# Differential attention as sixteen steps with the projections in between, and own PSUM banks for scores and transposes

## The chip, the cores and the metric

The kernel runs on one core of one Trainium2 chip. The metric is the device time of the whole program in microseconds (us), as the median of several executions. One core has five engines that work side by side, each through its own queue in order: TensorE (PE, matrix products and transposes), VectorE (DVE), ScalarE (ACT), GpSimd (POOL) and SyncE (SP, which issues the DMAs).

## The reference, cut to what matters

A transformer block with differential attention, latent attention, memory cross-attention and a mixture of experts is followed by a second block (gated delta rule, sliding-window attention, two feed-forward layers). There are 512 tokens of width 1024. The change lies in the first stage, the mixer of the first block:

```
h = rms_norm(x, norm_mix_g); proj = h @ w_in
q_d, k_d, v_d, c_q, c_kv, k_pe = split(proj)
lam = exp(sum(lq1 * lk1)) - exp(sum(lq2 * lk2)) + lambda_init
# differential attention: 8 heads, two score maps of width 32 per head
p = softmax(s1 + bias) - lam * softmax(s2 + bias)      # causal; bias is linear in the distance of the positions
diff_out = rms_norm(p @ v_d) * gain
# latent attention follows, from c_q, c_kv and k_pe
x = x + concat([diff_out, mla_out]) @ w_out
```

The keys and values of the memory attention (`w_mem_kv` on a normed memory of 256 rows) are projected in this stage too, and are read in the next one.

## The kernel before

Activations are held with features on the 128 partitions and 512 tokens along the free axis, in 8 chunks. A projection is a product in three parts (`mm3`, L399 to L401): activations and weights are each split into a high and a low part in a reduced 32-bit format (`hi`, `lo`, `xh`, `xl`; ACT makes the high part at L406, DVE the low part at L407), and three products are accumulated for each of 8 chunks, 24 matmuls for one block. A block of 128 output columns streams 512 columns in each matmul; a block of `w_v` or of the memory streams 256. The weights come in tiles of 512 KB, issued by SP as buffers come free. The accumulators of the projections (`mmp`) turn over in two banks of PSUM.

`mix()` runs first: `start` makes the split of the normed activations and the sums of squares (`sqt`, then `stp` on PE, `rt` on POOL, `stb` on PE, `rbc` on DVE). Then `MSEQ` lists the parts in program order: `p` projects a pair of query and key blocks (4 pairs), `v` half of the values, `c` and `k` the latent blocks, `r` the rope table, `n` the latent norms, `m` the memory's load, keys and values, and `h` (`attend(c)`) the differential attention of a pair of heads. One `attend` has four parts, i = 0 to 3, of 128 queries against (i+1)*128 keys. A part makes four score maps (`sc`, L1857, each on 32 rows of PE's array), takes their minimum against the distance on DVE (`s`, L1861), scales the minimum (`mnd`, L1866), takes the exponentials on ACT (L1870), joins two maps per head (L1874 to L1876), transposes the result on PE (`pt`, L2014), copies it on ACT (`pT`, L2016) and multiplies it with the values (`po`, L2006). After four parts the output is normed and transposed (`on`, L1888; `pt`, L1892).

What stands on each engine in which order is settled by a scheduler that places all instructions by its own estimate of their times, with program order as the priority. So parts that are listed one after the other can be mixed with each other. PSUM has 8 banks. In this part of the program two go to the projections, one to `po`, and five (`ps_d`) are shared by the score maps, by the transposes and by the first pair's two projections (`PQ`). The first of those five is the bank in which `start` has its sums.

Of the kernel before, what the change touches and what calls it, by code (L numbers as in the profile page):

```python
# [13 lines left out]
P = 128  # L14
# [13 lines left out]
MSEQ="v0 p1 v1 h0 r0 p2 c0 h1 c1 p3 h2 k1 k0 n0 m0 h3 m1 m2"  # L28
# [249 lines left out]
class K:  # L278
# [1440 lines left out]
    def mix(self):  # L1719
# [5 lines left out]
        with ExitStack() as st:  # L1725
# [20 lines left out]
            def qk(j):  # L1746

                ps = self.proj(d["w_qk"], j, hs, bank=ps_d.tile([P, T], F32, name="po", tag="s") if j in PQ else None)
# [5 lines left out]
                return t  # L1754
# [3 lines left out]
            def pair(c):  # L1758
                return qk(c), qk(c + 4)

            self.cst_load(mp, "mix")
            nxt = pair(0)
# [41 lines left out]
            pairs, cq, kms, cqs, mem = {0: nxt}, [], [], [], []  # L1804

            def latent_q(j):
                ps = self.proj(d["w_qk"], 8 + j, hs)
                t = F(f"cq{j}")
                V.tensor_tensor(t, ps, rbc, OP.mult)
                cq.append(t)  # L1810

            def latent_kv():
                ps = self.proj(d["w_qk"], 10, hs)
                t = F("ckv")
                V.tensor_tensor(t, ps, rbc, OP.mult)
                return t

            def rope_keys():
                ps = self.proj(d["w_qk"], 11, hs)
                kp = F("kp")  # L1820
                V.tensor_tensor(kp, ps, rbc, OP.mult)
                V.tensor_tensor(kp, kp, cs, OP.mult)
# [6 lines left out]

            def latent_norms():  # L1830
# [3 lines left out]
                V.scalar_tensor_tensor(mq, bq, -(96.0 ** -0.5), cs, op0=OP.mult, op1=OP.mult)  # L1834
                rkv, bkv = self.stats([ckv], 128, B)
# [5 lines left out]
                self.split(t[:, 0], t[:, 1], ckv, self.sm("mla_kv_norm_g"))  # L1841
                return mq, rkv, bkv, (t[:, 0], t[:, 1])

            def attend(c):

                q, k = pairs[c]
                slopes = [2.0 ** -(2 * c + a + 1) for a in range(2)]
                po = ps_o.tile([P, 4, 2, 64], F32, name="po", tag="po")
                mn, sm = Y("mnd", 16), Y("smd", 16)

                sm = sm.rearrange("p (m i a) -> p m i a", m=2, a=2)
                for i in range(4):
                    n = (i + 1) * P
                    sc = [ps_d.tile([P, T], F32, name="sc", tag="s")[:, :n] for m in range(4)]
                    for m in range(4):
                        r = slice(32 * m, 32 * m + 32)
                        nc.tensor.matmul(sc[m], q[r, i * P:n], k[r, :n], start=True, stop=True)  # L1857
                    es = []
                    for m in range(4):
                        s = w3.tile([P, T], F32, name="s", tag="s")[:, :n]  # L1860
                        V.tensor_tensor_reduce(s, sc[m], dist[i], 1.0, 3e38, OP.add, OP.min,  # L1861
                                               mn[:, 4 * i + m:4 * i + m + 1])
                        es.append(s)
                        if m % 2:
                            mi = mn[:, 4 * i + m - 1:4 * i + m + 1]
                            V.tensor_scalar(mi, mi, slopes[m // 2], None, op0=OP.mult)  # L1866
# [181 lines left out]
```

## Time and profile before

| what | us |
|---|---|
| median of three timed executions (2113.8 to 2115.72) | 2114.2 |
| the profiled execution, its own time | 2121.12 |
| its span, first to last instruction | 2118.9 |
| PE busy in the span | 2008.4 |
| the stretch of the differential attention, first projection to last product with the values (24.9 to 265.3) | 240.4 |
| PE busy in that stretch | 208.72 |

All times of rows are us from the span's start. In the profile, a PE row's length includes the time until its result is out, so the cost of one matmul in a sequence is read from start to start. The granted clock of PE is given as a share of full speed: 1.00 is the 2.4 GHz level, 0.50 the 1.2 GHz level.

### The profile page before, as it was taken

To read this page: it belongs to the slowest core of one execution; us is meant where nothing else is said; L and a number is where in the kernel's file an instruction comes from. 1 tells how busy PE (TensorE), PEld (TensorE's weight loads), DVE (VectorE), ACT (ScalarE), POOL (GpSimd) and SP (SyncE) were. 2 spreads that over 40 slices of the span, in tenths; PEclk is the share of its full clock that TensorE was granted. 3 is DMA by queue.
4 is the path that set the end of the run, shared out by engine and by line. 5 is a ranking of instruction groups with operands and counts; after the bars stand their busy time and mean duration, and the time that the engine had idled before them with its cause. 6 is when DMAs were issued, how large, how long until landed. Compare 5 with 4: busy or idle time off the path is not lost.

```text
span 2118.9 us, 26396 instructions
## 1 busy us (share of the span) xinstructions
PE 2008.4 (95%) x10094; PEld 1539.6 (73%) x10094; DVE 1036.4 (49%) x2115; ACT 739.9 (35%) x1453; POOL 343.6 (16%) x320
## 2 busy tenths in 40 slices
PE   5988799989999999999999899999999999999997
PEld 5767567877555556787887788888877678888887
DVE  6455474663222325778875643344345654334334
ACT  4335464452111113344553422222324543222221
POOL 2001124120000000244440211011111011101111
PEclk9877799999999998999999999999999999999999
DMA  4212211426988874211112232332231023233322
GB/s 155 80 40 60 75 41 51 154 68 223 383 287 331 331 279 159 71 60 41 53 38 80 89 98 77 114 93 88 88 100 50 21 89 91 87 92 110 100 76 74
DMA packets 75457, 243.44 MB, mean 115 GB/s; under 512 B 8824, under 2 KB 11968, under 8 KB 75328
## 3 DMA queue, kind: packets, MB, share of 16 engines
q1 hardware_dynamic: 73520, 240.34, 33.8%
q8 instruction: 81, 1.33, 0.3%
q10 hardware_dynamic: 1664, 1.34, 0.2%
q14 instruction: 48, 0.39, 0.1%
q0 software_dynamic: 144, 0.04, 0.0%
HBM read 235.36 MB, written 6.29 MB: 114 GB/s over the span
## 4 chain that ended last, share of the span: by engine, by line
PE 70%; DVE 3%; ACT 1%; POOL 1%; DMA 1%; issue 0%; DVEq 0%; ACTq 0%
PE mmp L399 16%; PE mmp L400 16%; PE mmp L401 15%; PE pgu L1548 6%; PE psx L1614 3%; PE py L1548 3%; PE pgt L1564 3%; PE sc L1327 1%; PE po L748 1%; PE tp L961 1%; PE po L1353 1%; PE sc L728 1%; PE pt L1339 0%; DVE cv L949 0%; POOL sqt L433 0%; PE pg L968 0%
## 5 line engine op out<-in xcount | busy, mean ns | idle before, releaser
L399 PE MATMUL mmp<-xh,hi 128*128 128x512 f32 (+1 forms) x1328 | 523.5, 394 | 1.9 <-DVE g L805 1.1
L400 PE MATMUL mmp<-xl,hi 128*128 128x512 f32 (+1 forms) x1328 | 517.3, 390 | 0.9 <-DVE xl L410 0.9
L401 PE MATMUL mmp<-xh,lo 128*128 128x512 f32 (+1 forms) x1328 | 517.2, 389 | 0.0
L406 ACT ACTIVATE hi<-raw 128x1024 fp32r<-128x1024 f32 (+2 forms) x256 | 252.6, 988 | 663.5 <-PE mmp L400 587.7
L407 DVE TENSOR_TENSOR lo<-raw,hi 128x1024 fp32r<-128x1024 f32 (+1 forms) x242 | 279.7, 1157 | 149.3 <-ACT hi L406 145.1
L399 PEld LDWEIGHTS mmp<-xh,hi 128*128 128x128 f32 x1328 | 253.4, 191 | 57.5 <-issue 4.5
L400 PEld LDWEIGHTS mmp<-xl,hi 128*128 128x128 f32 x1328 | 253.2, 191 | 51.9 <-issue 2.5
L401 PEld LDWEIGHTS mmp<-xh,lo 128*128 128x128 f32 x1328 | 252.7, 190 | 50.5 <-issue 1.0
L807 POOL TENSOR_TENSOR g<-g,rbc 128x512 f32<-128x512 f32 x44 | 75.2, 1708 | 508.8 <-ACT g L806 508.8
L399 PE MATMUL mmp<-ahi,hi 128*128 128x512 f32 (+1 forms) x374 | 141.9, 380 | 0.0
L400 PE MATMUL mmp<-alo,hi 128*128 128x512 f32 (+1 forms) x374 | 141.9, 380 | 0.0
L401 PE MATMUL mmp<-ahi,lo 128*128 128x512 f32 (+1 forms) x374 | 141.9, 379 | 0.0
L433 POOL TENSOR_TENSOR sqt<-sqt 128x512 f32<-128x512 f32 (+1 forms) x50 | 68.6, 1373 | 245.0 <-ACT sqt L429 228.2
L809 DVE TENSOR_TENSOR a<-mmp,g 128x512 f32<-128x512 f32 x44 | 30.4, 691 | 144.6 <-PE mmp L401 144.6
L805 DVE TENSOR_TENSOR g<-mmp,rbc 128x512 f32<-128x512 f32 x44 | 30.4, 691 | 112.8 <-PE mmp L401 112.7
L399 PEld LDWEIGHTS mmp<-ahi,hi 128*128 128x128 f32 x374 | 70.4, 188 | 14.1
L400 PEld LDWEIGHTS mmp<-alo,hi 128*128 128x128 f32 x374 | 70.4, 188 | 14.0
L401 PEld LDWEIGHTS mmp<-ahi,lo 128*128 128x128 f32 x374 | 70.4, 188 | 14.0
L1564 PEld LDWEIGHTS pgt<-G,tok 128*128 128x128 f32 x512 | 61.6, 188 | 10.9 <-issue 8.9
L1615 DVE TENSOR_TENSOR x<-psx,x 128x512 f32<-128x512 f32 x64 | 43.4, 688 | 47.1 <-PE psx L1614 46.3
L1564 PE MATMUL pgt<-G,tok 128*128 128x256 f32 x512 | 64.6, 282 | 1.0 <-ACT xl L1566 1.0
L1548 PE MATMUL pgu<-raw,xh 128*64 128x512 f32 x256 | 61.4, 611 | 3.3 <-PEq L1644 3.3
(513 smaller groups left out, 3053.3 us busy)
## 6 DMA issues: line engine op xcount, KB each, us to landing
raw<-in_w_egu_dram SPq DMA_DIRECT2D x128, 512.0 KB, 7.9
raw<-in_w_gu_dram SPq DMA_DIRECT2D x88, 512.0 KB, 3.5
raw<-in_w_ed_dram SPq DMA_DIRECT2D x64, 512.0 KB, 8.0
raw<-in_w_out_dram SPq DMA_DIRECT2D x24, 512.0 KB, 3.6
raw<-in_w_gdn_dram SPq DMA_DIRECT2D x24, 512.0 KB, 3.6
raw<-in_w_dn_dram SPq DMA_DIRECT2D x32, 384.0 KB, 3.0
raw<-in_w_dn_dram SPq DMA_DIRECT2D x32, 320.0 KB, 2.8
raw<-in_w_qk_dram SPq DMA_DIRECT2D x12, 512.0 KB, 4.2
```

The lines of the kernel that those rows point to most:

```text
L399: mm(ps, a[0], b[0], start=first, stop=False)
L400: mm(ps, a[0], b[1], start=False, stop=False)
L401: mm(ps, a[1], b[0], start=False, stop=last)
L406: nc.scalar.activation(hi, src, AF.Copy)
L407: (eng or nc.vector).tensor_tensor(lo, src, hi.bitcast(F32), OP.subtract)
L433: (nc.vector if i == len(chunks) - 1 else nc.gpsimd).tensor_tensor(acc, acc, s, OP.add)
L805: nc.vector.tensor_tensor(g, pg, bc, OP.mult)
L807: nc.gpsimd.tensor_tensor(g, g, bc, OP.mult)
L1548: nc.tensor.matmul(ps[hb], a[:, hb], w[b][:, o:o + 512], start=first, stop=last)
L1564: nc.tensor.matmul(pgt[:, 256 * j:256 * j + 256], toks[k][:, t, cs], G[:, t], start=k + t == 0, stop=k + t == 4)
L1614: nc.tensor.matmul(psx, ys[k][:, a, c * P:(c + 1) * P], ss[a], start=a + k == 0, stop=a + k == 2)
L1615: nc.vector.tensor_tensor(self.x[c], psx, self.x[c], OP.add)
```

## The change

Five things change, all in `mix()`.

The projections become generators (`g_blk`, `g_tok` and others) that yield after each chunk of three matmuls; a chunk of 512 columns counts one unit, one of 256 half a unit. The listed parts become `jobs`, taken one after the other by `fill(n)`, which runs n units; `ahead` loads the weights of the next job one job early.

The attention becomes 16 steps (4 pairs of heads by 4 parts). Each step of the loop transposes the step before, makes the scores of this step, runs 2 units, multiplies the step before with the values, and runs units up to `FILL=8` in all. `tc.issue_after(anchor[-1])` puts each chunk of a projection behind the last score map that was made ahead of it.

The banks of PSUM are dealt out anew: one to `po`, and this is now the bank in which `start` has its sums; one to all transposes (`ps_t`); four to the score maps (`ps_s`), in which the first pair is projected as well.

On DVE and ACT, the four minima of a step are scaled by one instruction with a table `slp`, and reciprocal and scaling of the sums are done for two heads at once. In the first two parts one bank and one copy take the transposes of both heads.

The order of the parts is new: values first, then rope table, pairs, latent blocks, latent norms, and the memory last.

```diff
-MSEQ="v0 p1 v1 h0 r0 p2 c0 h1 c1 p3 h2 k1 k0 n0 m0 h3 m1 m2"
+MSEQ="r0 p1 v1 p2 c0 c1 p3 k0 k1 n0 m0 m1 m2"
+FILL=8
...
-            ps_d = dst.enter_context(tc.tile_pool(name="ps_d", bufs=5, space=PSUM))
             ps_o = dst.enter_context(tc.tile_pool(name="ps_od", bufs=1, space=PSUM))
...
+            ps_t = dst.enter_context(tc.tile_pool(name="ps_td", bufs=1, space=PSUM))
+            ps_s = dst.enter_context(tc.tile_pool(name="ps_sd", bufs=4, space=PSUM))
...
+            def g_blk(w, hs, n=T, bank=None):
+                ps = bank or self.pmm.tile([P, T], F32, name="mmp", tag="mm")
+                for c in range(8):
+                    with ExitStack() as sa:
+                        if anchor:
+                            sa.enter_context(tc.issue_after(anchor[-1]))
+                        self.mm3(ps[:, :n], w(c, 0, P), hs[c], c == 0, c == 7)
+                    yield n / T
+                return ps[:, :n]
...
+            for x in range(2):
+                run(g_qk(pairs[0], x, 4 * x, self.load(d["w_qk"], 4 * x, 8), ps_s.tile([P, T], F32, name="sc", tag="sc")))
...
+                sc = [ps_s.tile([P, T], F32, name="sc", tag="sc")[:, :n] for m in range(4)]
...
+                anchor.append(z.ins)
...
+                mi = mn[:, 4 * i:4 * i + 4]
+                V.tensor_tensor(mi, mi, slp[:, 4 * c:4 * c + 4], OP.mult)
...
+                s0, s1 = sm[:, 0, i], sm[:, 1, i]
+                V.reciprocal(s1, s1)
+                V.scalar_tensor_tensor(s1, s0, nlam, s1, op0=OP.mult, op1=OP.mult)
+                for a in range(2):
+                    V.scalar_tensor_tensor(es[2 * a], es[2 * a + 1], s1[:, a:a + 1], es[2 * a], op0=OP.mult, op1=OP.add)
+                return c, i, [es[0], es[2]]
...
+            def turn(p, nk):
+
+                pt = ps_t.tile([P, T], F32, name="pt", tag="pt")
+                for a, x in enumerate(p):
+                    for k in range(nk):
+                        o = (a * nk + k) * P
+                        nc.tensor.transpose(pt[:, o:o + P], x[:, k * P:(k + 1) * P], I)
+                n = len(p) * nk * P
+                r = wk.tile([P, T], F32, name="pT", tag="pT", bufs=PB)
+                nc.scalar.activation(r[:, :n], pt[:, :n], AF.Copy)
+                return [r[:, a * nk * P:(a + 1) * nk * P] for a in range(len(p))]
...
+            run(g_tok(vd, self.load(d["w_v"], 0, 8), hs, rt, 0))
+            steps = [(c, i) for c in range(4) for i in range(4)]
+            last, done = None, []
+            for s_ in steps + [None, None]:
+                pT = []
+                if last:
+                    c, i, es = last
+                    pT = turn(es, i + 1) if i < 2 else turn(es[:1], i + 1)
+                now = scores(*s_) if s_ else None
+                fill(2)
+                if done:
+                    mixed(*done.pop())
+                if last:
+                    values(c, i, 0, pT[0])
+                    if i > 1:
+                        pT += turn(es[1:], i + 1)
+                        fill(2)
+                    values(c, i, 1, pT[1])
+                    if i == 3:
+                        done.append((c, normed(c)))
+                if s_:
+                    fill(FILL - (4 if last and last[1] > 1 else 2))
+                last = now
+            fill(1000)
```

The order that the scheduler makes of it, at three places. First PE's queue at the very start. Before, these are its first rows (`stp` is the sum of squares, `mmp` from `hi`, `xh` a block of the values):

```order
L2043 UNCONDITIONAL_BRANCH
L437 MATMUL stp<-ones,sqt 128x1 x4
L399 MATMUL mmp<-hi,xh 128x256 x2
L400 MATMUL mmp<-lo,xh 128x256
L401 MATMUL mmp<-hi,xl 128x256
L399 MATMUL mmp<-hi,xh 128x256
```

And now (`sc_226` and `sc_257` are the first pair's query and key blocks; 43 rows of theirs stand ahead of these):

```order
L401 MATMUL sc_226<-xl_130,hi_222 128x512
L402 MATMUL sc_226<-xh_129,lo_223 128x512
L400 MATMUL sc_257<-xh_129,hi_253 128x512
L401 MATMUL sc_257<-xl_130,hi_253 128x512
L402 MATMUL sc_257<-xh_129,lo_254 128x512
L438 MATMUL stp_165<-ones_87,sqt_142 128x1 x4
L400 MATMUL mmp_342<-hi_334,xh_119 128x256
L401 MATMUL mmp_342<-lo_335,xh_119 128x256
```

All 48 matmuls of the first pair have moved ahead of `stp`; before, they stood behind two blocks of the values.

The second place is PE's queue at the last two parts (i = 2 and 3) of the first pair of heads. Before:

```order
L2014 MATMUL pt_722<-cst_all_113,s_707 128x128 x3
L2014 MATMUL pt_736<-cst_all_113,s_712 128x128 x3
L1857 MATMUL sc_745<-qk_279,qk_248 128x512
L1857 MATMUL sc_746<-qk_279,qk_248 128x512
L1857 MATMUL sc_747<-qk_279,qk_248 128x512
L2006 MATMUL po_616<-vd0_312,pT_726 128x64
L2006 MATMUL po_616<-vd1_313,pT_726 128x64
L2006 MATMUL po_616<-vd2_314,pT_726 128x64
L1857 MATMUL sc_748<-qk_279,qk_248 128x512
L2006 MATMUL po_616<-vd0_312,pT_740 128x64
```

And now:

```order
L402 MATMUL mmp_665<-hi_563,xl_130 128x256
L1898 MATMUL sc_696<-qk_282,qk_251 128x512
L1898 MATMUL sc_697<-qk_282,qk_251 128x512
L1898 MATMUL sc_698<-qk_282,qk_251 128x512
L1898 MATMUL sc_699<-qk_282,qk_251 128x512
L400 MATMUL mmp_722<-hi_559,xh_119 128x256
L1926 MATMUL pt_690<-cst_all_113,s_610 128x128 x3
L401 MATMUL mmp_722<-lo_560,xh_119 128x256
L402 MATMUL mmp_722<-hi_559,xl_120 128x256
L400 MATMUL mmp_722<-hi_559,xh_119 128x256
```

Four score maps stand in a row and projections follow them; before, three stood together, the fourth came behind products with the values, and no projection stood between the parts.

The third place is PE's queue at the latent norms. Before (three sums `stp` and three rows `stb`, in the third pair of heads, here the first two of each):

```order
L437 MATMUL stp_1493<-ones_87,sqt_1488 128x1 x4
L1892 MATMUL pt_1113<-cst_all_113,on_1111 128x128 x4
L1857 MATMUL sc_1222<-qk_889,qk_856 128x128
L1857 MATMUL sc_1223<-qk_889,qk_856 128x128
L1857 MATMUL sc_1224<-qk_889,qk_856 128x128
L1857 MATMUL sc_1225<-qk_889,qk_856 128x128
L450 MATMUL stb_1502<-cst_all_113,rt_1498 128x128 x4
L437 MATMUL stp_1513<-ones_87,sqt_1511 128x1 x4
L450 MATMUL stb_1522<-cst_all_113,rt_1518 128x128 x4
```

And now:

```order
L1937 MATMUL po_1238<-vd0_315,pT_1189 128x64 x2
L1898 MATMUL sc_1648<-qk_1291,qk_1216 128x256
L1849 MATMUL psr_1441<-kp_1438,cst_mix_220 128x512
L438 MATMUL stp_1452<-ones_87,sqt_1447 128x1 x4
L1898 MATMUL sc_1649<-qk_1291,qk_1216 128x256
L1898 MATMUL sc_1650<-qk_1291,qk_1216 128x256
L1926 MATMUL pt_1259<-cst_all_113,s_1199 128x128 x2
L1926 MATMUL pt_1259<-cst_all_113,s_1203 128x128 x2
L1898 MATMUL sc_1651<-qk_1291,qk_1216 128x256
L451 MATMUL stb_1461<-cst_all_113,rt_1457 128x128 x4
L438 MATMUL stp_1472<-ones_87,sqt_1470 128x1 x4
```

The norms now stand among the scores of the fourth pair of heads, whose parts are drawn ahead of their turn, and the memory's keys follow them. On all engines the order behind this stage is the same but for a few places in the second block.

## Rows read from the trace of the kernel before

**Rows 1.** The page: PE's granted clock in 40 slices of the span (each 53 us), and from the DMA issues the load of one tile of weights (KB each, median us from issue to landing).

```profile
PEclk9877799999999998999999999999999999999999
...
raw<-in_w_qk_dram SPq DMA_DIRECT2D x12, 512.0 KB, 4.2
```

**Rows 2.** Busy time of the engines by stretch (start:end in us, length, then busy time and number of instructions of PE, its weight loads, DVE, ACT, POOL, then PE's granted clock, the DMA share and GB/s).

```profile
60.00:83.30 23.30, 23.30 (x153) 20.32 (x152) 9.37 (x31) 10.32 (x25) 0.00 (x0) 1.00 0.30 92
...
105.00:109.20 4.20, 4.20 (x11) 3.22 (x11) 2.07 (x7) 2.04 (x5) 0.00 (x0) 0.50 0.00 0
...
131.00:165.00 34.00, 25.51 (x102) 16.66 (x101) 17.79 (x63) 12.98 (x40) 0.00 (x0) 0.65 0.07 19
...
175.00:201.00 26.00, 21.08 (x111) 17.08 (x112) 14.40 (x56) 11.91 (x38) 7.59 (x9) 0.61 0.20 61
201.00:228.00 27.00, 27.00 (x221) 25.08 (x219) 14.54 (x34) 15.25 (x30) 6.02 (x4) 1.00 0.38 119
228.00:265.30 37.30, 23.29 (x107) 15.36 (x108) 19.24 (x68) 15.34 (x45) 3.96 (x2) 0.70 0.16 49
...
24.90:265.30 240.40, 208.72 (x1118) 166.34 (x1119) 121.19 (x350) 100.35 (x236) 24.16 (x21) 0.82 0.21 65
```

**Rows 3.** What PE waited for between 20 and 266 us (us in total, times, longest).

```profile
PE pt L2014 <- DVE s L1876: 15.4, 11, 3.6
PE po L2006 <- ACT pT L2016: 6.8, 6, 1.7
PE pt L2014 <- DVE mnd L1866: 3.2, 1, 3.2
PE stb L450 <- POOL rt L418: 2.7, 2, 1.7
```

**Rows 4.** The start, in order of time (start us, us, engine, line, operation, count; in brackets the idle time before it and what ended it): the first weights' high part, the last low parts of the activations, the sum of squares on PE, and the first matmul of the first pair.

```profile
5.79 1.06 ACT L406 ACTIVATE hi<-raw 128x1024 fp32r<-128x1024 f32 x1
...
17.68 4.09 DVE L410 SCALAR_TENSOR_TENSOR xl<-x,smt,xh 128x512 fp32r<-128x512 f32 x3
...
23.22 1.87 PE L437 MATMUL stp<-ones,sqt 128*128 128x1 f32 x8 [23.22 <-DVE sqt L433]
...
34.29 0.40 PE L399 MATMUL po<-xh,hi 128*128 128x512 f32 x1
```

**Rows 5.** PE's pace, in order of time (same columns): two matmuls of 256 columns at the start, the first and the last of eight in a row of 512 columns, and transposes, score maps, matmuls of 256 columns and products with the values at the third pair of heads. A score map and a product with the values are two instructions each.

```profile
25.95 0.41 PE L399 MATMUL mmp<-hi,xh 128*128 128x256 f32 x1
...
26.16 0.41 PE L400 MATMUL mmp<-lo,xh 128*128 128x256 f32 x1
...
109.99 0.39 PE L399 MATMUL mmp<-xh,hi 128*128 128x512 f32 x1
...
111.58 0.40 PE L400 MATMUL mmp<-xl,hi 128*128 128x512 f32 x1
...
204.49 0.49 PE L2014 MATMUL pt<-cst_all,s 128*128 128x128 f32 x3
204.91 1.13 PE L1857 MATMUL sc<-qk 32*128 32x512 f32 x6
205.97 0.38 PE L399 MATMUL mmp<-xh,hi 128*128 128x256 f32 x1
206.19 0.28 PE L400 MATMUL mmp<-xl,hi 128*128 128x256 f32 x1
206.31 0.28 PE L401 MATMUL mmp<-xh,lo 128*128 128x256 f32 x1
...
207.51 1.45 PE L2006 MATMUL po<-vd,pT 128*128 128x64 f32 x12
208.88 1.12 PE L1857 MATMUL sc<-qk 32*128 32x512 f32 x2
```

**Rows 6.** The scores of part i = 2 and then the last part (i = 3) of the fourth pair of heads, in order of time (same columns), down to the last product with the values and the first scores of the latent attention.

```profile
241.06 1.66 PE L1857 MATMUL sc<-qk 32*128 32x384 f32 x8
...
250.74 2.09 PE L1857 MATMUL sc<-qk 32*128 32x512 f32 x8
...
252.85 0.69 DVE L1861 CUSTOM_DVE_ANT_0 s<-sc,dist 128x512 f32<-128x512 f32 x1 [3.54 <-PE sc L1857]
...
254.39 0.72 ACT L1870 ACTIVATE s<-s,mnd 128x512 f32<-128x512 f32 x1 [3.00 <-DVE mnd L1866]
...
257.30 1.09 PE L2014 MATMUL pt<-cst_all,s 128*128 128x128 f32 x4 [3.64 <-DVE s L1876]
...
263.61 1.97 PE L2006 MATMUL po<-vd,pT 128*128 128x64 f32 x8 [0.75 <-ACT pT L2016]
...
273.52 0.61 PE L1965 MATMUL sc<-km,qm 128*128 128x128 f32 x4
```

**Rows 7.** DVE's small instructions of the attention between 23 and 282 us, by line and shape (count, busy us, mean ns, idle before).

```profile
L1866 DVE TENSOR_SCALAR mnd<-mnd 128x2 f32<-128x2 f32 x32 | 7.7, 240 | 0.6
L1875 DVE SCALAR_TENSOR_TENSOR smd<-smd,ls 128x1 f32<-128x1 f32 x32 | 6.9, 219 | 1.0
...
L1874 DVE RECIPROCAL smd<-smd 128x1 f32<-128x1 f32 x32 | 5.1, 161 | 16.6 <-ACT s L1870 16.2
```

**Rows 8.** The latent norms and the memory's norm on PE, first sum and last row, in order of time (same columns as rows 4).

```profile
174.27 0.95 PE L437 MATMUL stp<-ones,sqt 128*128 128x1 f32 x8
...
192.53 1.18 PE L450 MATMUL stb<-cst_all,rt 128*128 128x128 f32 x4
```

More of the change, by code (lines that the diff above doesn't have):

```diff
@@ L1828, in rope_keys, with g_mem_key, g_mem_value @@
                     nc.scalar.activation(kms[k][64:], psr[64:], AF.Copy)
+            def g_mem_key(t, j, i, w):
+                ps = yield from g_blk(w, mem[0], 256)
+                V.tensor_tensor(t[:, i * 256:i * 256 + 256], ps, mem[2], OP.mult)
+                if i:
+                    nc.sync.dma_start(self.kv1d[0][:, (j - 1) * 256:(j + 1) * 256], t)
+            def g_mem_value(out, u, w):
+                yield from g_tok(out, w, mem[0], mem[1], u)
+                if u:
+                    for t in range(2):
+                        nc.sync.dma_start(self.kv1d[1][:, t * 512:(t + 1) * 512], out[t])
             def latent_norms():
@@ new lines, in values, with normed @@
+            def values(c, i, a, pT):
+                if (i, a) == (0, 0):
+                    pos_[c] = ps_o.tile([P, 4, 2, 64], F32, name="po", tag="po")
+                for k in range(i + 1):
+                    h = 2 * c + a
+                    nc.tensor.matmul(pos_[c][:, i, a], pT[:, k * P:(k + 1) * P], vd[k][:, h * 64:(h + 1) * 64],
+                                     start=k == 0, stop=k == i)
+            def normed(c):
+                pf = pos_[c].rearrange("p i a b -> p (i a) b")
@@ L1889, in attend, with mixed @@
                                 rr.unsqueeze(2).to_broadcast([P, 8, 64]), OP.mult)
-                pt = ps_d.tile([P, 512], F32, name="pt", tag="s")
+                return on
+            def mixed(c, on):
+                pt = ps_t.tile([P, 512], F32, name="pt", tag="pt")
                 for i in range(4):
@@ new lines, in mix @@
+                if k == "m" and j == 0:
+                    jobs.append((None, lambda: mem.extend(self.mem_load(d["memT"], "norm_mem_g"))))
+                if k == "m" and j == 1:
+                    for u in range(4):
+                        jobs.append((L("w_mem_k", u), lambda w, u=u: g_mem_key(mk(u), u, u % 2, w)))
+                if k == "m" and j == 2:
+                    for u in range(2):
+                        jobs.append((L("w_mem_v", u), lambda w, u=u: g_mem_value(mv(), u, w)))
@@ new lines, in mix, with mk, mv, ahead @@
+            mkt, mvt = {}, []
+            def mk(u):
+                if u // 2 not in mkt:
+                    mkt[u // 2] = B("mk")
+                return mkt[u // 2]
+            def mv():
+                if not mvt:
+                    mvt.extend(B("mv") for t in range(2))
+                return mvt
+            cur, held = [None], []
+            def ahead():
+                for k, (load, job) in enumerate(jobs):
+                    if load:
+                        if not held:
+                            held.append(load())
+                        return
@@ new lines, in fill @@
+            def fill(n):
+                while n > 0:
+                    if cur[0] is None:
+                        if not jobs:
+                            return
+                        load, job = jobs.pop(0)
+                        if load is None:
+                            job()
+                            continue
+                        w = held.pop() if held else load()
+                        cur[0] = job(w)
+                        ahead()
+                    try:
+                        n -= next(cur[0])
+                    except StopIteration:
+                        cur[0] = None
@@ L1922, in mix @@
+            fill(1000)
+            mq, rkv, bkv, (ckh, ckl) = lat
             dst.close()
```

139 lines of the change are left out of this document (66 added, 73 removed).

## The prediction

> **What bounds the kernel now.** I read PE's clock over the whole span first: it is at 0.9 or more in all but a few slices, and the low ones (7, 7, 7, 8) lie in the first 270 us [rows 1]. Then the stretches of that stage: from 24.9 us, the first projection, to 265.3 us, the last product with the values, PE is busy for 208.7 of 240.4 us at a mean clock of 0.82, while DVE has 121 us of work and ACT 100 [rows 2]. So no engine is full, and PE is both late and slow. Where it is slow is plain by stretch: 60 to 83.3 and 201 to 228 us, where projections stand among the parts of the attention, run at 1.00 without a gap; 131 to 165, 175 to 201 and 228 to 265.3, where scores, transposes and products with the values follow each other with few projections, run at 0.61 to 0.70 (between the levels of 1.2 and 2.4 GHz), with gaps [rows 2]. The gaps wait for the exponentials' join on DVE (15.4 + 3.2 us), for the copy of the transposes on ACT (6.8) and for the latent norms (2.7) [rows 3]. One part shows the chain: scores at 250.74, minima at 252.85, exponentials at 254.39, first transposes at 257.30 [rows 6]. Ahead of all this PE does nothing until 23.2 us [rows 4].
>
> PE's work in that stretch at 2.4 GHz, from start to start: seven matmuls of 512 columns take 1.59 us, 0.227 each; one of 256 takes 0.12; three transposes with one change of kind take 0.42, so 0.11 each; three 512-column score maps side by side 1.06, and the fourth, which stands alone, has a row of 1.12 again; six products with the values 1.37, 0.228 each; a change of kind costs about 0.1 (0.22 instead of 0.12 behind the scores) [rows 5]. Counted over the order: 303 x 0.227 = 68.8; 384 x 0.12 = 46.1; scores 17.0, since most groups are split three and one; 96 transposes 10.1; 80 products 18.2; the small matmuls of the norms 6.9 (an estimate from their rows, 0.25 each); 124 changes 12.4. Sum 179.5. The stage loses 240.4 - 179.5 = **60.9 us**: some 31 by waits (28.1 of them in [rows 3]), the rest to the lower clock.
>
> **The change part by part.**
>
> *The start.* The first pair's 48 matmuls wait today although their weights' high part is made at 5.8 us [rows 4]: their banks are those in which `start` has its sums, so they come after the statistics, at 34.29. Now `po` takes that bank, and the 48 stand ahead of `stp` in the queue. That removes 48 x 0.227 = 10.9 us from behind 24.9, if they end by 23.2. The last low part of the activations is done at 21.8 us [rows 4]; from 7 us on, even at the pace of 1.2 GHz (0.21 for 256 columns [rows 5], so 0.43 for 512) 48 take 20.5 us and would end at 27.5; at the full pace they are fed by DVE and end near 22.5. Behind them is `stp`, and behind that the values. I take 0.5 us late. And PE is then awake: today some 28 matmuls of the values run at 0.21 instead of 0.12 (2.6 us); I leave 1 of that. Loss here 1.5 (0 to 5).
>
> *Scores in four banks.* Twelve of the sixteen groups now stand four in a row; scores fall from 17.0 to 15.1 us. With the first pair gone and one change less, PE's work from 24.9 us is 179.5 - 10.9 - 1.9 - 0.5 = 166.2.
>
> *Steps with 8 units between.* Pairs, values and latent blocks are 96 units, so exactly twelve steps have theirs: 24 x 0.227 = 5.4 us of projections and on average 2.7 of its own work, 8.1 us a step. The chain that must fit: at i = 3 it took 6.56 us from scores to first transposes, with scores at the lower clock [rows 6]. Now all four minima (two more, 0.69 each) and all four exponentials (two more, 0.72 each) come before the join: 6.56 + 2.8 - 1.0 for scores at full pace (2.09 to 1.06, [rows 5, 6]) = 8.4 us. In the order PE has 8.9 us of work between that step's scores and its transposes in the first pair of heads, and from the second on a step's transposes stand behind the scores of one or two later steps. So it is covered, by 0.5 us in the worst step. If that cover went, what a step costs is under the rivals. The stretch 60 to 83.3 is the nearest row for such a mixture and lost nothing; I take 2 us for the twelve (0 to 19).
>
> *Fewer small instructions.* 16 each of the scaling, the joining factor and the reciprocal fall away: 16 x (0.24 + 0.22 + 0.16) = 9.9 us of DVE [rows 7]. DVE is not what ends; it falls from 121 to about 111 us in a stage of some 195. Nothing by itself.
>
> *One bank for all transposes.* A transpose waits for the copy of the one before. PE waited for copies 6 times, at most 1.7 us [rows 3]. Inside the twelve steps projections stand between; behind them I count it in the tail.
>
> *Latent norms and the tail.* Here the units end. From the scores of the fourth pair's first step to the first memory key PE has 17 us of work and no projection. Today the norms take from 174.27 to 193.7 us [rows 8], 19.4 us, for 9.6 us of PE's work at a clock of 0.61 [rows 2]: 9.8 lost. In the new order the same three round trips over DVE and POOL stand among four steps of scores, whose banks come free only as DVE takes the minima; DVE has some 20 us of work there (an estimate from the order: minima, joins, the memory's splits and the copies of the norms, 0.2 to 0.8 us each), and it also waits three times for POOL and twice for the exponentials, some 2 us each. I take 33 us, twice PE's work as today: loss 16 (10 as today, 26 if each trip is waited for in full). Behind it keys and values of the memory, 24 us of projections, stand among the last transposes. Getting back to 2.4 GHz costs about 2, half of 4.2 us that projections ran at 0.50 behind such a stretch [rows 2], and the last four products, each behind its own copy, some 5.5. Loss 7.5 (3 to 12).
>
> *Loads and SP.* The same tiles in nearly the same order, 4.2 us each [rows 1] against 5.4 us for a unit job; the next is loaded a job ahead. Hidden; where a tile came late, PE would stop with all behind it. POOL's eight small writes of `slp` stand in idle time before 7 us.
>
> **Sum.** Losses 1.5 + 2 + 16 + 7.5 = 27. The last product with the values ends at 24.9 + 166.2 + 27 = 218.1 instead of 265.3, so 47.2 us earlier. From there to the first scores of the latent attention it takes 8.2 us today [rows 6] and ends in slow matmuls; 30 matmuls and four transposes now, 7.2: one more. What follows is the same order behind the same chain, and moves along whole. So 48 us: 2121.1 - 48 = 2073 for a profiled execution. That one was 0.3% above the median of 2114.2; the saved us are carried over as they are: **2066**.
>
> **The rivals.**
>
> *Better than that*: the norms hide behind keys and values after all. Losses of 9 in all would give 24.9 + 166.2 + 9 = 200, 65 earlier, one more behind: 2048. For it: DVE's 20 us there would nearly fit into PE's 17. Against: in today's order that same chain slowed PE to 0.61 [rows 2]. Chance 0.18.
>
> *DVE's chain paces the steps.* Where no projection stands between, a part took 9.7 us (241.06 to 250.74 for i = 2, the next scores [rows 6]); DVE also has one split of weights in most steps, in front of some minima. If steps took 9.7 instead of 8.1, 12 x 1.6 = 19 us go: 2085. It decides where the minima of a step are not done when the next scores want their four banks. Chance 0.17.
>
> *Only the start and the banks work*, the rest waits as today in other places: 10.9 + 1.9 + 1.5 = 14 us, 2100. The queue as built speaks against it: projections do stand between. Chance 0.05.
>
> *Slower: the clock stays at its lower level.* 131 to 165 us shows PE at 0.65 with scores, transposes and products in small pieces [rows 2]. The change puts such pieces into every stretch of projections. If PE were held at 1.2 GHz through the twelve steps, their 98 us of work would take 196: 98 - 48 = 50 us slower, 2164. It is slower than before from half of these steps on. Against it: 201 to 228 us, with transposes, scores and products among the blocks, stayed at 1.00, as did 60 to 83.3 [rows 2]. Here the Trainium skill speaks against the change ("TensorE: Matmul & The Clock Gate", Part 4: PE-mode transpose): transposes do not count as busy for the clock in the way that matmuls do. By that rule the clock would fall as in this rival; the two stretches at 1.00 speak for its being too little here to matter. Chance 0.06.
>
> **How the numbers follow.** Forecast, 2052 to 2080 around 2066: 0.54; better 0.18; DVE 0.17; only the start 0.05; slower 0.06. Differences under 0.2%, 4 us, cannot be told from no change by a measurement here. Faster by more: 0.54 + 0.18 + 0.17 + 0.05 less a little of the last two: 0.92; same 0.02; slower 0.06. The range takes in the forecast, better and DVE with the bounds of the steps and the norms: 2045 to 2090.
>
> **What would show it.** PE starts matmuls by 8 us, and the first values follow `stp` at about 25. From 35 to 135 us PE has no gap over 1 us and a granted clock of 1.00; DVE's and ACT's waits for PE there don't matter. From about 135 to 168 us the clock is near 0.6 and PE waits for the minima and for POOL's `rt`. The last product with the values ends near 218, the latent attention's first scores follow 7 us later, and every later mark is 48 us earlier. Wrong it would be by a clock below 0.9 before 130 us, by waits of PE for DVE in the first twelve steps, or by later stages that do not move along.

## The result, and the profile after

The changed kernel takes 2050.9 us as the median of four executions (2050.69 to 2053.69), the kernel before on the same chip 2114.4 (2113.8 to 2115.72): a ratio of 0.9702, 95% interval 0.9685 to 0.9719, so 63.5 us saved where 48 were forecast. The time lies in the range, next to that of the rival "better than that" (2048), but not for that rival's reason.

The page of the changed kernel: busy time of each engine and PE's clock in 40 slices, which answer to [rows 1].

```profile
PE 1984.0 (97%) x10094; PEld 1521.2 (74%) x10094; DVE 1024.5 (50%) x2067; ACT 735.6 (36%) x1445; POOL 347.7 (17%) x328
...
PEclk9988999999999999999999999999999999999999
```

What PE waited for from the start to 225 us (us in total, times, longest), which answers to [rows 3]:

```profile
PE sc L400 <- ACT hi L407: 7.1, 1, 7.1
PE sc L1898 <- DVE mnd L1903: 2.3, 1, 2.3
PE po L1937 <- ACT pT L1929: 1.3, 1, 1.3
PE pt L1958 <- DVE rrd L1947: 1.0, 1, 1.0
PE sc L401 <- DVE xl L411: 0.5, 1, 0.5
...
```

The waits for the join (15.4 + 3.2 us) are gone, and those for the copy fell from 6.8 to 1.3 us. The first row, 7.1 us, is the time before PE's first matmul. What is lost now is lost mostly to the clock. By stretch (columns as in [rows 2]): the values and the twelve steps; from the fourth pair's first scores to the first memory key; the part of that in which PE has no gap; from the first memory key to the end of the last product with the values; the first 5 us of that; and all of it.

```profile
24.42:131.55 107.13, 105.77 (x664) 86.08 (x663) 73.98 (x209) 58.95 (x144) 6.82 (x7) 1.00 0.27 84
131.55:162.77 31.22, 27.96 (x103) 18.86 (x103) 18.11 (x57) 15.42 (x44) 8.64 (x10) 0.57 0.15 51
136.34:162.77 26.43, 26.43 (x86) 17.64 (x87) 14.37 (x47) 10.63 (x31) 8.01 (x9) 0.50 0.17 60
162.77:203.29 40.52, 40.47 (x307) 37.93 (x306) 16.77 (x36) 20.54 (x40) 10.08 (x5) 0.95 0.40 124
162.77:168.00 5.23, 5.23 (x31) 5.23 (x31) 1.10 (x4) 0.60 (x1) 0.00 (x0) 0.61 0.01 3
24.42:203.29 178.87, 174.20 (x1071) 142.88 (x1070) 108.85 (x302) 94.91 (x227) 25.54 (x21) 0.91 0.27 88
```

The marks in PE's timeline that answer to [rows 4, 6, 8]: the first matmul of the first pair, the last at the lower clock and the next one, the first sum, the first three matmuls of the values, the first scores of the fourth pair, the first memory key, the last product with the values, the first scores of the latent attention.

```profile
7.11 0.80 PE L400 MATMUL sc<-xh,hi 128*128 128x512 f32 x1 [7.11 <-ACT hi L407]
...
16.03 0.63 PE L400 MATMUL sc<-xh,hi 128*128 128x512 f32 x1
16.45 0.50 PE L401 MATMUL sc<-xl,hi 128*128 128x512 f32 x1
...
23.62 0.95 PE L438 MATMUL stp<-ones,sqt 128*128 128x1 f32 x8
...
24.42 0.37 PE L400 MATMUL mmp<-hi,xh 128*128 128x256 f32 x1
24.63 0.28 PE L401 MATMUL mmp<-lo,xh 128*128 128x256 f32 x1
24.75 0.28 PE L402 MATMUL mmp<-hi,xl 128*128 128x256 f32 x1
...
131.55 0.50 PE L1898 MATMUL sc<-qk 32*128 32x128 f32 x8
...
162.77 0.56 PE L400 MATMUL mmp<-xh,hi 128*128 128x256 f32 x1
...
202.19 1.10 PE L1937 MATMUL po<-vd,pT 128*128 128x64 f32 x8
...
211.63 0.61 PE L2095 MATMUL sc<-km,qm 128*128 128x128 f32 x4
```

The latent attention's first scores come 273.52 - 211.63 = 61.9 us earlier. The two profiled spans differ by 67.0 us, the medians by 63.5; of the extra in the spans some 2 us lie where the experts' stage begins. There PE's clock was 0.82 from 455 to 475 us in the execution before and is 0.98 at the same work from 393 to 410 us now. What follows the stage moved along nearly whole.

### The profile page after: what moved, and what is told of

Same layout as the page of the kernel before. It is cut to its first block, busy times and chain, and to the rows that moved or that the text cites. A ratio compares the mean times of both kernels' runs of the same rounds, so it can differ in the third digit from the quotient of the medians.

```text
span 2051.9 us, 26341 instructions
## 1 busy us (share of the span) xinstructions
PE 1984.0 (97%) x10094; PEld 1521.2 (74%) x10094; DVE 1024.5 (50%) x2067; ACT 735.6 (36%) x1445; POOL 347.7 (17%) x328
## 4 chain that ended last, share of the span: by engine, by line
PE 72%; DVE 3%; DMA 1%; ACT 1%; POOL 1%; issue 0%; DVEq 0%; ACTq 0%
PE mmp L400 16%; PE mmp L401 16%; PE mmp L402 16%; PE pgu L1549 6%; PE psx L1615 3%; PE py L1549 3%; PE pgt L1565 3%; PE sc L1328 1%; DMA raw<-in_w_swa_dram 1%; PE po L749 1%; DVE lo L408 1%; PE tp L962 1%; PE po L1354 1%; PE pt L1340 0%; DVE cv L950 0%; PE sc L729 0%
## 5 line engine op out<-in xcount | busy, mean ns | idle before, releaser
L1565 PEld LDWEIGHTS pgt<-G,tok 128*128 128x128 f32 x512 | 61.6, 188 | 10.9 <-issue 8.9
L1549 PE MATMUL py<-raw,act 128*64 128x512 f32 x256 | 63.9, 599 | 0.2
```

The source lines that it names most:

```text
L1549: nc.tensor.matmul(ps[hb], a[:, hb], w[b][:, o:o + 512], start=first, stop=last)
L1565: nc.tensor.matmul(pgt[:, 256 * j:256 * j + 256], toks[k][:, t, cs], G[:, t], start=k + t == 0, stop=k + t == 4)
```

## The experiments

"Saved" is the difference of the medians against the kernel before on the same chip (medians 2113.4 to 2116.2 us there); the changed kernel saves 63.5.

| run | median us | ratio, 95% | saved us |
|---|---|---|---|
| old order, start's bank alone | 2097.3 | 0.989 to 0.9927 | 18.9 |
| old order, all new banks | 2076.7 | 0.9786 to 0.9827 | 39.5 |
| new order, start's bank undone | 2064.2 | 0.972 to 0.9767 | 52.0 |
| new order, five shared banks | 2053.3 | 0.9701 to 0.9733 | 60.2 |
| new order, 16 units a step | 2075.8 | 0.9791 to 0.983 | 40.4 |
| new order, 7 units a step | 2051.2 | 0.9672 to 0.9715 | 63.8 |
| new order, small instructions apart | 2049.4 | 0.968 to 0.9712 | 64.1 |
| eight wide products added | 2059.1 | 0.9669 to 0.9772 | 54.4 |
| the same again | 2044.0 | 0.965 to 0.9698 | 70.9 |
| memory's part in two | 2042.0 | 0.9638 to 0.967 | 71.5 |
| memory's part in two, 7 units | 2043.3 | 0.9636 to 0.9678 | 71.7 |
| memory's part in two, four wide products | 2045.0 | 0.9652 to 0.9685 | 69.3 |

### The start and the banks

The old order with only the statistics' bank given to `po`:

```diff
-            ps_d = dst.enter_context(tc.tile_pool(name="ps_d", bufs=5, space=PSUM))
             ps_o = dst.enter_context(tc.tile_pool(name="ps_od", bufs=1, space=PSUM))
+            ps_d = dst.enter_context(tc.tile_pool(name="ps_d", bufs=5, space=PSUM))
```

> The kernel before with one edit: the one bank for the products with the values is dealt out first, so that it and no longer a score bank is the one of the start's sums. The first pair's 48 matmuls then stand ahead of the first sum. Theory (the gain is the start plus projections between the steps): the start alone saves 48 x 0.227 = 10.9 us plus up to 2.6 of the half pace behind it, so 2101 (2099 to 2104). Rival (the banks bring most of it): the first pair is done earlier, its parts can stand among the projections that follow, and more than 25 us go: below 2089.

18.9 us, 5 more than the 13.5 (10.9 + 2.6) expected of the start and less than the rival's 25. In the two traces 16.6 us of it are there by the latent attention's first scores (256.92 against 273.52). That the scheduler, with the first pair done early, places the projections better among the first parts is a reading and not shown: the kernel before has projections there too. All new banks, in the old order:

```diff
-            ps_d = dst.enter_context(tc.tile_pool(name="ps_d", bufs=5, space=PSUM))
             ps_o = dst.enter_context(tc.tile_pool(name="ps_od", bufs=1, space=PSUM))
+            ps_t = dst.enter_context(tc.tile_pool(name="ps_td", bufs=1, space=PSUM))
+            ps_s = dst.enter_context(tc.tile_pool(name="ps_sd", bufs=4, space=PSUM))
...
-                        self.av(es[2 * a], i + 1, ps_d, wk, vd, po[:, i, a], 2 * c + a, "s")
+                        self.av(es[2 * a], i + 1, ps_t, wk, vd, po[:, i, a], 2 * c + a, "s")
```

> The kernel before with the new banks alone: one for the products with the values (the start's), one for all transposes, four for the scores; the parts in their old order, the small instructions as before. Theory (projections between the steps bring the larger half): in the built order only the first five or six parts have projections among them, the rest follow each other bare; 2085 (2075 to 2095), so some 30 of the 63 us. Rival (own banks are the change, the written-out order adds nothing): 2060 or less. Rival (one bank for all transposes costs what the start gives, since in this order no projection covers the copies): 2105 or more.

39.5 us, better than the middle of what was expected. With free score banks the scheduler mixes projections into the parts by itself. What it still lacks is seen at the end of this kernel. Its stretches from 165 us, and from PE's timeline the wait for the third pair's output, two transposes and the last two products with the values:

```profile
165.00:195.00 30.00, 30.00 (x183) 22.46 (x182) 20.25 (x49) 13.87 (x36) 8.42 (x4) 1.00 0.46 145
195.00:228.00 33.00, 21.66 (x97) 16.93 (x97) 8.24 (x25) 11.11 (x26) 1.64 (x1) 0.57 0.00 0
```

```profile
205.88 1.11 PE L1893 MATMUL pt<-cst_all,on 128*128 128x128 f32 x4 [4.57 <-DVE on L1889]
...
220.87 1.06 PE L2015 MATMUL pt<-cst_all,s 128*128 128x128 f32 x4
222.68 1.97 PE L2007 MATMUL po<-vd,pT 128*128 128x64 f32 x8 [0.75 <-ACT pT L2017]
224.44 1.06 PE L2015 MATMUL pt<-cst_all,s 128*128 128x128 f32 x4
226.25 1.97 PE L2007 MATMUL po<-vd,pT 128*128 128x64 f32 x8 [0.75 <-ACT pT L2017]
```

All projections are used up at 194 us, and the last scores are done at 197; the fourth pair's transposes and products follow bare, each behind its copy, at 0.57. Of the 33 us, 21.66 x 0.57 = 12.3 are work at 2.4 GHz, so 20.7 are lost. That is most of the 24 by which the changed kernel is faster than this one, though the two also differ elsewhere: at the latent norms the old order loses less, some 9 us (130 to 165 us at 0.76) against some 16. In the changed kernel the same products stand among the memory's and the latent projections, and PE is busy for 40.47 of 40.52 us.

The other way round, the new order with the old place of the start's bank:

```diff
-            ps_o = dst.enter_context(tc.tile_pool(name="ps_od", bufs=1, space=PSUM))
-            ps_t = dst.enter_context(tc.tile_pool(name="ps_td", bufs=1, space=PSUM))
             ps_s = dst.enter_context(tc.tile_pool(name="ps_sd", bufs=4, space=PSUM))
+            ps_o = dst.enter_context(tc.tile_pool(name="ps_od", bufs=1, space=PSUM))
+            ps_t = dst.enter_context(tc.tile_pool(name="ps_td", bufs=1, space=PSUM))
```

> The changed kernel with the banks dealt out in the old order: the score banks first, so that the first pair's projections wait for the start's sums again. Theory: the 48 matmuls come back behind 24.9 us, 10.9 us plus up to 2.6 for the half pace of the values: 2062 to 2065. Rival (PE has slack behind the start in the norms' stretch, which takes it up): 2051 to 2055.

11.5 us less saved, within what was expected for the start. In the two traces a row of the experts' stage (the first `pl` from `xl`) is 8.4 us later (407.77 against 399.41), so some 3 of the 11.5 arose behind that and are not explained. And the new order with five banks shared by scores and transposes:

```diff
-            ps_t = dst.enter_context(tc.tile_pool(name="ps_td", bufs=1, space=PSUM))
-            ps_s = dst.enter_context(tc.tile_pool(name="ps_sd", bufs=4, space=PSUM))
+            ps_t = ps_s = dst.enter_context(tc.tile_pool(name="ps_sd", bufs=5, space=PSUM))
...
```

> The changed kernel with its steps as they are, but five banks shared again by scores, transposes and the first pair's projections; the products with the values keep the start's bank. The earlier run with the new banks in the old order of the parts gave 39.5 of the 63.5 us. Theory (banks and written order each bring a part of their own: start 13, banks some 20 to 26, order some 25): without own banks the shared order falls back by the banks' part, 2070 (2066 to 2076). Rival (the two do the same thing, they bring projections between the parts, and either is enough once the start is right): 2051 to 2056, since the built order still has projections between the steps.

60.2 us: the theory of two separate parts falls, the rival holds. Own banks are worth 3 us in the written order and some 20 in the old one (39.5 - 18.9); both do the same thing, they bring projections between the parts. The written order was run only as a whole: what the order of the parts, the steps and `issue_after` each bring was not taken apart.

### How many projections between two steps

```diff
-FILL=8
+FILL=16
```

> The changed kernel with 16 units of projections between two steps instead of 8: they run out after about six steps, the norms and the memory's projections stand behind those, and the last seven or eight steps have nothing between them. Theory (projections between the steps cover the chain and keep the clock): a bare step costs 9.3 us (37.3 us for the fourth pair's four parts before) for 2.7 us of work at 2.4 GHz, so up to 8 x 6.6 = 53 us are lost again: 2095 (2080 to 2105). Rival (the deeper pipeline of the written-out steps is enough, each step's transposes behind the next step's scores): bare steps cost their work at the lower clock, 5.4 us, 8 x 2.7 = 22: 2072. Rival (the cover is worth nothing): 2051.

40.4 us saved, 23 less than with 8. The number is close to the first rival's (2072), the place is only in part. Stretches of this kernel: steps with next to no projections, steps with few (15 matmuls of 512 columns), and its end.

```profile
105.00:120.00 15.00, 11.59 (x56) 6.86 (x54) 11.92 (x38) 7.33 (x21) 2.56 (x1) 0.74 0.12 36
184.00:198.00 14.00, 14.00 (x80) 8.79 (x77) 7.95 (x31) 8.14 (x28) 3.43 (x2) 1.00 0.33 110
200.00:226.00 26.00, 15.92 (x70) 13.41 (x69) 6.73 (x19) 8.92 (x19) 1.64 (x1) 0.52 0.00 1
```

The steps at 184 to 198 us lose nothing with so little between them; those at 105 to 120 us wait 3.4 us and run at 0.74. Most of what this kernel loses against the changed one is again at the fourth pair's products at the end: 26 - 15.92 x 0.52 = 17.7 us. With 7 units instead:

```diff
-FILL=8
+FILL=7
```

> The changed kernel with 7 units between two steps instead of 8, so that one and a half steps of the fourth pair still have projections and the norms stand behind those. Theory (the stretch without projections is what is lost now, some 14 us for the 17 us of PE's own work in it): with about 11 us of own work there it loses 9 to 11, so 2047 (2044 to 2051). Rival (the cover of 7 units is too short for the chain over DVE and ACT, 8.4 us against 8.2): waits appear in the twelve steps, 2053 to 2060.

No difference, so the theory's 4 us did not come. In its trace the stretch of the norms loses less to the clock (140.8 to 163.4 us at 0.91), but PE waits there for the memory's sum on DVE and POOL. The latent attention's first scores come 9.5 us earlier (202.16 against 211.63), its end only 2.8: the first matmul behind it stands at 266.81 instead of 269.57. Where the rest goes is not shown.

### The small instructions

```diff
-                V.tensor_tensor(mi, mi, slp[:, 4 * c:4 * c + 4], OP.mult)
+                for a in range(2):
+                    V.tensor_scalar(mi[:, 2 * a:2 * a + 2], mi[:, 2 * a:2 * a + 2], 2.0 ** -(2 * c + a + 1), None, op0=OP.mult)
...
-                V.reciprocal(s1, s1)
-                V.scalar_tensor_tensor(s1, s0, nlam, s1, op0=OP.mult, op1=OP.mult)
                 for a in range(2):
+                    V.reciprocal(s1[:, a:a + 1], s1[:, a:a + 1])
+                    V.scalar_tensor_tensor(s1[:, a:a + 1], s0[:, a:a + 1], nlam, s1[:, a:a + 1], op0=OP.mult, op1=OP.mult)
```

> The changed kernel with the small instructions of DVE as before: scaling of the minima, reciprocal and joining factor for each head apart, 48 more instructions, 16 x (0.24 + 0.22 + 0.16) = 9.9 us of DVE. Theory (DVE has room, nothing of it shows): 2051 (2048 to 2054). Rival (DVE's chain paces the steps, or at least the four of the norms): up to 9.9 us, 2055 to 2061.

64.1 us saved, as without the edit. In the changed kernel these rows of DVE come to 3.5 + 2.7 + 2.6 = 8.8 us, here to 7.8 + 5.2 + 5.0 = 18.0; the 9.2 us show nowhere. The built order also shifts a little, so a gain or loss of 1 or 2 us stays open.

### The clock in the stretch of the norms

```diff
-                sc = [ps_s.tile([P, T], F32, name="sc", tag="sc")[:, :n] for m in range(4)]
+                full = [ps_s.tile([P, T], F32, name="sc", tag="sc") for m in range(4)]
+                sc = [t[:, :n] for t in full]
...
+                    if c == 3 and m in (1, 3):
+                        nc.tensor.matmul(full[m], I, dist[3], start=True, stop=True)
                     z = nc.tensor.matmul(sc[m], q[r, i * P:n], k[r, :n], start=True, stop=True)
```

> The changed kernel with work added for nothing: in the fourth pair of heads, ahead of two of the four score maps of each step, a product of 512 columns that nobody reads is put into the bank of that map, eight in all, each some 0.9 us at 2.4 GHz by the row of psr (half of its 2.08 us at 0.50). In the trace 31.2 us go by from this pair's first scores to the first memory key, for 17.0 us of work; from 136.3 us on PE has no gap, but its granted clock is 0.50. Theory (this stretch is slow because the clock stays low with nothing but small pieces on PE): the wide products bring the clock back, 17 + 7.2 us of work and some 3 of waits, so 27 instead of 31: 2047 (2043 to 2052). Rival (the round trips over DVE and POOL pace it): the added work hides or comes on top, with the clock as low as now: 2051 to 2065.

Neither theory covers this: two executions took 2046.0 and 2049.8 us, as the theory had it, and two 2068.3 and 2068.4, above both ranges. The wide products do not bring the clock back in every execution. The same kernel was run again:

> The kernel with the eight wide products that nobody reads once more, unchanged, since its four executions fell into two groups: 2046.0 and 2049.8 us (mean granted clock 0.986 and 0.985), 2068.3 and 2068.4 (0.977 both); the profile was of the latter, with the clock at 0.50 from 141 to 181 us. Theory (the same queue runs at either level in the norms' stretch, and that alone makes the two times): again two groups, near 2048 and 2068; where a profile is of the faster one, 141 us on is at 1.00 and the first memory key is some 18 us earlier than the 181.4 of the slower one. Rival (something else moves, a DMA or the order of waits): times in between, or a slower execution with the clock up.

2043.7, 2043.7, 2044.0, 2045.0 and one of 2053.2. The first group came again, the second did not, and one execution lies in between, with a mean clock of 0.984 between the 0.977 of the slow pair and the 0.988 to 0.989 of the short ones in this run. This time the profile is of a short execution. The same stretch of the same queue, first of the profiled execution of 2068.4 us, then of that of 2043.7:

```profile
132.00:141.00 9.00, 8.25 (x36) 4.26 (x34) 7.62 (x23) 7.34 (x18) 1.09 (x2) 0.96 0.01 2
141.00:181.00 40.00, 40.00 (x108) 21.94 (x108) 13.44 (x46) 11.23 (x35) 6.93 (x9) 0.50 0.13 40
```

```profile
132.00:141.00 9.00, 8.31 (x39) 4.37 (x38) 8.21 (x24) 6.71 (x17) 1.02 (x3) 1.00 0.01 2
141.00:161.60 20.60, 20.43 (x104) 11.82 (x105) 12.28 (x43) 11.23 (x35) 7.73 (x8) 1.00 0.26 78
```

From 141 us to the first memory key (181.39 and 161.65) PE is busy with no gap but one of 0.17 us, for 40.4 us at 0.50 or for 20.6 at 1.00. So in this kernel PE's clock makes the whole difference, and the round trips over DVE and POOL fit into the shorter time. How much the changed kernel, which has no useless products to fill PE's time, would win by a clock at 1.00 there is not shown. With the clock up, a kernel with eight useless products of 1.06 us each is 7 us faster than the changed one.

### The memory's part in two

The split of the memory comes first, its sum of squares last, and the sums stand in score banks; so the memory's keys don't wait for the norms.

```diff
-MSEQ="r0 p1 v1 p2 c0 c1 p3 k0 k1 n0 m0 m1 m2"
+MSEQ="r0 p1 v1 p2 c0 c1 p3 k0 k1 m0 n0 q0 m1 m2"
...
-                _, bq = self.stats(cq, 256, B)
+                _, bq = self.stats(cq, 256, B, ps=bank())
...
-                    jobs.append((None, lambda: mem.extend(self.mem_load(d["memT"], "norm_mem_g"))))
+                    jobs.append((None, lambda: mem.extend(self.mem_load(d["memT"], "norm_mem_g", True))))
+                if k == "q":
+                    jobs.append((None, lambda: mem.extend(mem.pop()(bank()))))
```

> The changed kernel with the memory's part taken in two: its split into high and low parts first, the three norms' sums in score banks instead of those of the projections, the memory's sum of squares last. In the built order 40 matmuls of the memory's keys then stand among the norms and the fourth pair's steps, where now there is no projection. Theory (the stretch from 131.5 to 162.8 us loses 14.2 us for want of projections): most of it comes back, less the wait for the split, some 3 to 5: 2041 (2037 to 2046). Rival (the round trips pace it, or the norms in the score banks hold the scores up): 2049 to 2058.

71.5 us saved, 8 more than the changed kernel: the theory holds, and this version beats both kernels. Its clock in the stretch, and behind it that of the kernel in which four useless wide products are added to the first step (the last edit below):

```profile
131.50:145.00 13.50, 10.16 (x60) 8.44 (x60) 8.63 (x25) 8.92 (x23) 4.85 (x6) 0.75 0.05 9
145.00:162.00 17.00, 16.26 (x106) 13.04 (x105) 12.17 (x34) 9.55 (x26) 4.31 (x5) 0.83 0.42 149
```

```profile
131.50:145.00 13.50, 13.50 (x80) 9.50 (x79) 8.92 (x28) 9.60 (x28) 4.38 (x6) 1.00 0.06 10
145.00:162.00 17.00, 15.56 (x94) 12.69 (x94) 13.16 (x32) 8.34 (x21) 4.15 (x5) 0.76 0.43 148
```

With 7 units a step:

> The kernel that takes the memory's part in two (2042.0), with 7 units between two steps instead of 8. Theory (what is left of the loss is the wait for the memory's split, some 9 us behind the last projection from the first activations, in which PE has only one step's small pieces): with a step and a half more of own work behind that projection the wait is covered: 2036 (2032 to 2041). Rival (the stretch is as long as the norms' round trips, wherever it stands): 2042 to 2047.

The same as with 8, as the rival had it. With the wide products:

```diff
...
+                    if (c, i) == (3, 0):
+                        nc.tensor.matmul(full[m], I, dist[3], start=True, stop=True)
                     z = nc.tensor.matmul(sc[m], q[r, i * P:n], k[r, :n], start=True, stop=True)
```

> The two last edits together: the memory's part taken in two (8 units a step), and products of 512 columns that nobody reads ahead of the four score maps of the fourth pair's first step alone, four of them, 1.06 us each from start to start where the clock was up. There PE waits 1.07 us for the normed output and 2.26 for the minima in the trace of the kernel with the memory in two, and its granted clock is 0.75 behind that, from 131.5 to 145 us. Theory (what comes ahead of the norms decides the level in them): the four hide in the 3.3 us of waits but for about 1, and the clock stays up, 13.5 x 0.25 = 3.4 us and as much again from 145 to 162 us (17 x 0.17 = 2.9) are won: 2037 (2034 to 2041). Rival (the clock falls later all the same): 2042 to 2046.

The rival again: the clock stays up to 145 us, as the theory had it, and beyond, but it falls behind a wait of 1.44 us for the memory's squares, which ends at 152.39, and no time is won. That the wait is what lets it fall is not shown.

## Why the prediction was right, and where it was off

The prediction counts 166.2 us of PE's work from 24.9 us on, and 17.0 of them up to the first memory key. The same count, split at the same marks, puts 108.2 ahead of the fourth pair's first scores and 41.0 behind the first memory key; these two are estimates. The third column is the measured length less the count, the fourth what the trace itself shows as gaps and as lower clock.

| term | loss predicted | length less the count | lost by the trace |
|---|---|---|---|
| start | 1.5 | 24.42 - 24.9 = -0.5 | -0.5 |
| values and twelve steps | 2 | 107.1 - 108.2 = -1.1 | 107.13 - 105.77 = 1.4, clock 1.00 |
| norms | 16 | 31.2 - 17.0 = 14.2 | 3.3 of gaps + 26.43 x 0.50 = 16.5 |
| tail | 7.5 | 40.5 - 41.0 = -0.5 | 5.23 x 0.39 + 0.05 of gaps = 2.1 |
| sum | 27 | 12.1 | 19.5 |

The last product ends at 203.3 us instead of 218.1. The forecast was right in kind: what is lost is waits and clock, and projections between the parts take both away. It was 15 us short in size. Some 7 of these are the count of PE's work, which was too high in all three stretches (some 159 by the trace instead of 166.2; which of its terms is too large is not shown), 5.4 are the tail, and 2 the start.

- **Start: right.** The 48 matmuls begin at 7.11. Seventeen run some 0.43 apart or slower, and from 16.79 on they are 0.23 apart. The sum comes at 23.62, 0.4 us late where 0.5 was taken. Undoing it costs 11.5 us. The 1 us left for a cold start of the values is not there: their matmuls are 0.12 apart from the second on.
- **Twelve steps: right**, and a little better: clock 1.00, and PE waits 1.3 us in all, once, for a copy. That DVE's chain would pace them is refuted by the trace and by the run with 9.2 us more of DVE.
- **Small instructions, one bank for transposes: right.** The fewer instructions bring nothing that can be measured, and the one bank costs that single wait for a copy.
- **Norms: right in size, wrong in what waits.** The prediction has PE waiting for the minima and for `rt`. It waits once for minima (2.26) and once ahead of the transposes of the third pair's output (1.00, put down to DVE's `rrd`), and for `rt` never. From 136.34 us on it has no gap and runs at 0.50, which is 13.2 us of the 16.5. That the sum came out near 16 is in part luck: waits and clock were taken together as "twice PE's work", and it was mostly clock.
- **Tail: the term that failed.** 7.5 us were taken and 2.1 lost. "the last four products, each behind its own copy, some 5.5" holds for the kernels whose projections are used up (0.64 to 0.75 us a copy in the runs with the old order and with 16 units). Here 15 projections of the latent attention stand among them and no copy is waited for. The 2 us for getting the clock back came as taken: from 162.77 to 168 us the clock is 0.61, with eleven matmuls 0.21 apart, and behind that 1.00. The count could have told: its 303 matmuls of 512 columns are twelve blocks of 24 and these 15.
- **What follows: nearly right.** From the last product's end to the latent attention it takes 8.3 us where 7.2 were counted. Before, it took 7.9: the last product's row ends at 263.61 + 1.97 = 265.6 and not at 265.3 as taken ahead of the prediction. So the one microsecond more did not come.
- **The rivals.** "Better" came true in its number only: its norms did not hide, its tail did. "Only the start and the banks" was priced at 14 us by what the banks remove; they bring 39.5, since the scheduler uses them. "Slower" did not come: the clock was 1.00 in all twelve steps.

On the rule quoted there from the Trainium skill ("TensorE: Matmul & The Clock Gate", Part 4: PE-mode transpose), that transposes do not count as busy for the clock as matmuls do: the stretch at 0.50 without a gap holds ten transposes of 128 columns among scores, sums and products with the values, and no projection, which agrees. It does not tell transposes from the other small pieces, and the same pieces ran at 1.00 from 141 to 161.6 us in the second run with wide products.

## What to carry to other kernels

Where scores, transposes and small products follow each other, keep some projections back for the last of them: by the trace of the old order with the new banks, some 20 of the 63 us here were won where it had run out of them. A few between two steps were enough in the run with 16 units, and none was too little. Look at who owns a bank at the very start: one bank in the wrong place held 48 ready matmuls back; undoing it cost 11.5 us. And read the granted clock beside the gaps: a stretch without a gap at 0.50 is as lost as one that waits half of the time.

## What the runs showed of the hardware

One queue ran at either level. With the same instructions, 8.25 or 8.31 of 9 us busy ahead and almost no gap behind, PE's clock was at 0.50 for 40 us in one execution and at 1.00 in another, 2068.4 against 2043.7 us. What decides between them is open: but for a shift of the whole by 0.6 us, nothing in PE's rows from 132 us to the fall differs by more than tenths of a microsecond. And a product of 512 columns of full 32-bit values takes 1.06 us from start to start at 1.00 (132.05 to 133.11), where one in the reduced format takes 0.23 (16.79 to 17.02 in the changed kernel).
